# Recurrent layer: scans and gated products in hand-written order on VectorE, four copies moved to ScalarE and four casts to GpSimd

## The chip, the cores and the metric

The kernel runs on one NeuronCore of a Trainium2 chip. The metric is the device time of one execution in microseconds (us), median of repeated runs. The core has TensorE (PE; PEld is its weight loading), VectorE (DVE), ScalarE (ACT), GpSimd (POOL) and SyncE (SP, which here only issues DMAs). Each engine takes its own instructions strictly in order; semaphores hold an instruction until what it reads is written and what it overwrites is free.

## The reference, cut to what matters

Two residual layers on a sequence of 512 tokens by 1024 features: a hybrid layer (state space and attention), then the recurrent layer, each followed by a squared-ReLU MLP. The change lies in the recurrent layer alone:

```python
gate, xr = zf[..., :LRU_WIDTH], zf[..., LRU_WIDTH:]          # z = u @ rec_w_in
xc = conv(xr)                                                # width 4, depthwise
for direction in range(2):
    r = sigmoid(blockdiag(xc, ra_w[direction]) + ra_b[direction])
    i = sigmoid(blockdiag(xc, ix_w[direction]) + ix_b[direction])
    log_a = -LRU_C * r * softplus(-lam[direction])
    a = exp(log_a)
    b = sqrt(-expm1(2.0 * log_a)) * (i * xc)
    h = scan(a, b, reverse=(direction == 1))                 # h_t = a_t h_(t-1) + b_t
    hs.append(h)
y = (hs[0] + hs[1]) * gelu(gate)
mix = y @ rec_w_out
```

## The kernel before

Activations lie feature by token: a tile has 128 features (partitions) by 512 tokens, so the layer's 1024 features are eight tiles. Every matmul operand is split into a rounded part (`hi`, or `wh` for weights) and a remainder (`lo`, `wl`), and each product is three matmuls: wh times hi (L586), wh times lo (L587), wl times hi (L588); for the small gate products these are L559 to L561. A weight block `wr` of 128x1024 comes by DMA; `wtile` makes `wh` from it on the engine that `self.hi_eng` names at that moment (GpSimd, L520, or ScalarE, L522) and `wl` on VectorE (L523).

The layer works on two groups of four feature tiles, g = 0 and 1. For each tile: convolution (L1470 on GpSimd, then L1472 on VectorE), split (L1477 to L1480), four gate products on TensorE, ScalarE's Tanh, Exp, Tanh and Square (L1506 to L1513) and two VectorE steps (L1514, L1515). When the four tiles of a group are through, `roots` takes their square roots on ScalarE (L1528), which needs another table of functions than Tanh, and for each tile on VectorE: a product (L1530), a forward scan into `hs` (L1533), a backward scan in place into `ti` (L1534), their sum (L1535). `behind(...)` keeps ScalarE from starting the roots ahead of the last gate function of the fourth tile.

While this goes on, TensorE computes the other columns of the input projection. Those of the gate branch for group 0 stand in the four `ps` banks until `raw` takes them (four copies on VectorE, L1591); then `ps` is computed again for group 1's gate branch. `branch` applies Gelu on ScalarE (L1545). `merge` makes, for each of four tiles, the gated product on VectorE (L1554), its rounded copy on ScalarE (L1555, into a tile `a`) and the remainder on VectorE (L1556, into a tile `ti`). Two feature tiles share one `a` and one `ti`, and these are the buffers of group 1's scans: four of each exist, so the first pair of merged tiles can only be written when tile 0's scans of group 1 have been read, the second pair after tile 1, and so on.

The eight merged tiles, in four pairs `ys`, are the moving operands of the output projection `wout`. TensorE takes them pair by pair: one pair is a chunk of 24 matmuls (4 outputs x 2 tiles x 3), a first half of the outputs is 4 chunks, and the rest follows. The first pair is written `a_7800`, `ti_7801` in the program before and `a_7795`, `ti_7796` after it; the second `a_7808`, `ti_7809` and `a_7813`, `ti_7814`.

The order of each engine's instructions is set by a scheduler that knows an estimated duration of each; only inside `manual_schedule` is an engine's order that of the code. Before, the roots and merges are left to the scheduler.

Of the kernel before, what the change touches and what calls it, by code (L numbers as in the profile page):

```python
# [11 lines left out]
F32 = mybir.dt.float32  # L12
F32R = mybir.dt.float32r
I32 = mybir.dt.int32
AF = mybir.ActivationFunctionType
ALU = mybir.AluOpType
# [3 lines left out]
P = 128  # L20
# [40 lines left out]
class Kern:  # L61
# [1372 lines left out]
    def rglru(self, u, h, win, gw, wout, g1, s, sh):  # L1434
# [4 lines left out]
        with ExitStack() as ctx:  # L1439
# [84 lines left out]
            def roots(g, gt, after):  # L1524

                with behind(after):
                    for a, th, ti in gt:
                        last = (A.activation(th, th, AF.Sqrt, scale=0.25),)  # L1528
                for o, (a, th, ti) in enumerate(gt):
                    V.tensor_tensor(ti, ti, th, op=ALU.mult)  # L1530
                    hs = self.tl(rp, "hs", [P, 512], bufs=8)
                    a, ti = both(a), both(ti)
                    V.tensor_tensor_scan(hs, a[:, 0], ti[:, 0], 0.0, op0=ALU.mult, op1=ALU.add)  # L1533
                    V.tensor_tensor_scan(ti[:, 1, ::-1], a[:, 1, ::-1], ti[:, 1, ::-1], 0.0, op0=ALU.mult, op1=ALU.add)  # L1534
                    V.tensor_tensor(hs, hs, ti[:, 1], op=ALU.add)  # L1535
                    hfs[g * 4 + o] = hs
                return last
# [10 lines left out]
            def merge(g, gg):  # L1548

                for o in range(4):  # L1550
                    if o % 2 == 0:
                        hi2, lo2 = (both(self.tl(rp, t, [P, 1024], F32R, bufs=4)) for t in ("a", "ti"))
                    hi, lo = hi2[:, o % 2], lo2[:, o % 2]
                    V.tensor_tensor(tok(gg[o]), tok(gg[o]), perm(hfs[g * 4 + o]), op=ALU.mult)  # L1554
                    A.copy(hi, gg[o])  # L1555
                    V.tensor_tensor(lo, gg[o], hi.bitcast(F32), op=ALU.subtract)  # L1556
                    ys.append((hi, lo))
# [11 lines left out]
            for g in range(2):  # L1569
# [16 lines left out]
                if g == 0:  # L1586
                    xps = [fetch(4 + o, ps[o], None, None) for o in range(4)]
                    last = roots(0, gt, last)
            raw = [self.tl(rp, t, [P, 512], bufs=2) for t in ("xh", "xl") * 2]
            for o in range(4):  # L1590
                V.tensor_copy(raw[o], ps[o])  # L1591
            self.hi_eng = None
            ps = self.lin(win, u, 512)
            last = roots(1, gt, last)
            gg, last = branch(raw, last, raw)
            merge(0, gg)
            gg, last = branch(ps, last)
            merge(1, gg)
# [188 lines left out]
```

## Time and profile before

| | us |
|---|---|
| median of 3 runs (1228.93 to 1230.33) | 1229.25 |
| the profiled execution: its own time | 1232.16 |
| its span, first to last instruction | 1230.4 |
| PE busy / DVE / ACT / POOL in the span | 1156.2 / 790.8 / 538.9 / 167.3 |

The rows of the trace are in the section of rows below. Times in them are counted from the span's start. The recurrent layer runs from about 687 to 870 us; between 760 and 820 us TensorE has idle time, and its granted clock falls there, while it is busy nearly all of the time on both sides.

### The profile page before, as it was taken

How to read it: one execution, taken by the hardware profiler on the slowest of the kernel's cores; microseconds unless marked ns; L12 is line 12 of the kernel's file. 1: busy time of each engine (PE TensorE's matmuls, PEld its weight loads, DVE VectorE, ACT ScalarE, POOL GpSimd, SP SyncE). 2: the span in 40 equal slices, each digit the busy share in tenths (PEclk: the TensorE clock that was granted, in tenths of full speed). 3: DMA queues.
4: the chain of work that ended last, by engine and by line, in shares of the span. 5: the costliest groups of instructions: out<-in, count | busy, mean ns of one | idle time of the engine just before them, and what ended most of it. 6: DMA issues, size and time to landing. Idle time of an engine off the chain costs nothing.

```text
span 1230.4 us, 17016 instructions
## 1 busy us (share of the span) xinstructions
PE 1156.2 (94%) x6584; PEld 970.9 (79%) x6584; DVE 790.8 (64%) x1223; ACT 538.9 (44%) x929; POOL 167.3 (14%) x239
## 2 busy tenths in 40 slices
PE   4898889899999999999999998889999999999997
PEld 2687667668988888888889986669988888888886
DVE  6586988997789765486333799885744323344243
ACT  4356787663543412233323369934534211343230
POOL 2449883200000000000000261000000000000000
PEclk8998889999999999999999999889999999999999
DMA  9421020356277676475322422132232332332311
GB/s 351 159 65 61 23 73 32 130 172 229 70 251 260 208 239 204 145 251 187 101 87 69 138 86 69 35 98 72 86 105 88 101 103 89 100 103 87 102 35 69
DMA packets 85905, 151.76 MB, mean 123 GB/s; under 512 B 5696, under 2 KB 34368, under 8 KB 85824
## 3 DMA queue, kind: packets, MB, share of 16 engines
q1 hardware_dynamic: 85824, 150.67, 37.4%
q8 instruction: 51, 0.84, 0.3%
q14 instruction: 30, 0.25, 0.1%
HBM read 148.55 MB, written 2.10 MB: 122 GB/s over the span
## 4 chain that ended last, share of the span: by engine, by line
PE 75%; DVE 14%; ACT 5%; issue 2%; POOL 2%; DMA 1%; SPq 0%; DVEq 0%; POOLq 0%; ACTq 0%
PE ps L587 13%; PE ps L588 13%; PE ps L586 13%; PE px L586 8%; PE px L588 8%; PE px L587 8%; DVE wl L523 2%; PE p L748 1%; PE po L1045 1%; DVE ti L1534 1%; DVE actb L459 1%; DVE hs L1533 1%; ACT pexp L1028 1%; PE p L587 1%; PE p L586 1%
## 5 line engine op out<-in xcount | busy, mean ns | idle before, releaser
L523 DVE TENSOR_TENSOR wl<-wr,wh 128x1024 fp32r<-128x1024 f32 (+1 forms) x169 | 205.1, 1215 | 272.5 <-ACT wh L522 265.7
L522 ACT CAST wh<-wr 128x1024 fp32r<-128x1024 f32 (+1 forms) x161 | 165.8, 1030 | 419.9 <-PE ps L587 200.4
L587 PE MATMUL ps<-actb,wh 128*128 128x512 f32 (+1 forms) x512 | 181.3, 354 | 0.1
L586 PE MATMUL ps<-acta,wh 128*128 128x512 f32 (+1 forms) x328 | 116.6, 356 | 0.0
L588 PE MATMUL ps<-acta,wl 128*128 128x512 f32 (+1 forms) x328 | 116.3, 355 | 0.0
L586 PE MATMUL ps<-hid,wh 128*128 128x512 f32 x288 | 112.1, 389 | 0.0
L588 PE MATMUL ps<-hid,wl 128*128 128x512 f32 x288 | 112.0, 389 | 0.0
L587 PE MATMUL ps<-hid,wh 128*128 128x512 f32 x288 | 112.0, 389 | 0.0
L587 PEld LDWEIGHTS ps<-actb,wh 128*128 128x128 f32 x512 | 97.5, 190 | 13.4 <-DVE actb L905 0.3
L586 PE MATMUL px<-hid,wh 128*128 128x512 f32 (+1 forms) x288 | 98.9, 343 | 0.0
L587 PE MATMUL px<-hid,wh 128*128 128x512 f32 (+1 forms) x288 | 98.5, 342 | 0.0
L588 PE MATMUL px<-hid,wl 128*128 128x512 f32 (+1 forms) x288 | 98.5, 342 | 0.0
L587 PE MATMUL px<-actb,wh 128*128 128x512 f32 (+1 forms) x224 | 85.5, 382 | 0.0
L668 DVE SCALAR_TENSOR_TENSOR acc<-wr,cact,acc 128x1024 f32<-128x1024 f32 x49 | 62.8, 1282 | 20.1 <-DMA wr<-ada_w 19.8
L588 PEld LDWEIGHTS ps<-acta,wl 128*128 128x128 f32 x328 | 62.8, 191 | 8.5
L586 PEld LDWEIGHTS ps<-acta,wh 128*128 128x128 f32 x328 | 62.7, 191 | 8.4
L586 PE MATMUL ps<-actc,wh 128*128 128x512 f32 (+1 forms) x184 | 65.1, 354 | 0.0
L588 PE MATMUL ps<-actc,wl 128*128 128x512 f32 (+1 forms) x184 | 64.8, 352 | 0.0
L587 PEld LDWEIGHTS ps<-hid,wh 128*128 128x128 f32 x288 | 54.1, 188 | 11.3
L588 PEld LDWEIGHTS ps<-hid,wl 128*128 128x128 f32 x288 | 54.0, 188 | 11.2
L586 PEld LDWEIGHTS ps<-hid,wh 128*128 128x128 f32 x288 | 54.1, 188 | 11.2
L587 PEld LDWEIGHTS px<-hid,wh 128*128 128x128 f32 x288 | 54.6, 190 | 6.3
(524 smaller groups left out, 2582.8 us busy)
## 6 DMA issues: line engine op xcount, KB each, us to landing
wr<-w SPq DMA_DIRECT2D x128, 512.0 KB, 3.7
wr<-ada_w SPq DMA_DIRECT2D x56, 512.0 KB, 4.4
wr<-wout SPq DMA_DIRECT2D x16, 512.0 KB, 3.7
araw<-ada_w SPq DMA_DIRECT2D x32, 256.0 KB, 3.0
wr<-win SPq DMA_DIRECT2D x16, 512.0 KB, 3.8
wr<-win SPq DMA_DIRECT2D x8, 384.0 KB, 6.0
h<-xT SPq DMA_DIRECT2D x8, 256.0 KB, 6.2
acta<-ada_w SPq DMA_DIRECT2D x8, 256.0 KB, 5.6
```

What stands on the lines that cost most here:

```text
L459: V.tensor_tensor_scan(*z, 0.0, op0=ALU.mult, op1=ALU.add)
L522: nc.scalar.copy(hi, src)
L523: (lo_eng or nc.vector).tensor_tensor(lo, src, hi.bitcast(F32), op=ALU.subtract)
L586: mm(out, wh, xh, start=first and a == a0 and lead(o), stop=False, skip_group_check=True)
L587: mm(out, wh, xl, start=False, stop=False, skip_group_check=True)
L588: mm(out, wl, xh, start=False, stop=last and a == a0 + kk - 1, skip_group_check=True)
L668: nc.vector.scalar_tensor_tensor(acc, raw, self.ca[:, k:k + 1], acc, op0=ALU.mult, op1=ALU.add)
L748: self.nc.tensor.matmul(ps[o:o + 32, 0:raws[k].shape[1]], self.ca[:, k:k + 1].to_broadcast([P, 32]), raws[k], start=k < 4, stop=k >= 4, sk ...
L1028: self.exp = nc.scalar.activation(p, s, AF.Exp, bias=nb, scale=r, accum_out=self.esum[:, h, t:t + 1])
L1045: self.nc.tensor.matmul(po[h2 * 64:h2 * 64 + 64, t * 128:(t + 1) * 128], self.vp[:, kb, p // 2], pts[h2][:, kb * 128:(kb + 1) * 128], star ...
L1533: V.tensor_tensor_scan(hs, a[:, 0], ti[:, 0], 0.0, op0=ALU.mult, op1=ALU.add)
L1534: V.tensor_tensor_scan(ti[:, 1, ::-1], a[:, 1, ::-1], ti[:, 1, ::-1], 0.0, op0=ALU.mult, op1=ALU.add)
```

## The change

- `roots` no longer issues the square roots (they are now lines of their own, L1588 for group 0 and L1597 for group 1) and writes its VectorE steps inside `manual_schedule` for VectorE: tile by tile, product, scan, scan, sum, in this order. After each tile of group 1 it calls `merge` for one tile of group 0 that came one place earlier.
- `merge` does one tile a call. The fourth tile of group 0 and all four of group 1 are merged behind the loop, outside of the hand-written order.
- The four copies of `ps` into `raw` are on ScalarE (L1592) and not on VectorE (L1591).
- `self.lin(win, u, 512)` is called ahead of `self.hi_eng = None`, so the casts of its four weight blocks are made on GpSimd (L520) and not on ScalarE (L522).
- Group 0's Gelu is issued ahead of group 1's scans in the code.

```diff
-            def roots(g, gt, after):
-
-                with behind(after):
-                    for a, th, ti in gt:
-                        last = (A.activation(th, th, AF.Sqrt, scale=0.25),)
-                for o, (a, th, ti) in enumerate(gt):
-                    V.tensor_tensor(ti, ti, th, op=ALU.mult)
...
+            def roots(g, gt, then=lambda o: None):
+
+                with self.tc.manual_schedule(engines={mybir.EngineType.DVE}):
+                    for o, (a, th, ti) in enumerate(gt):
+                        V.tensor_tensor(ti, ti, th, op=ALU.mult)
+                        hs = self.tl(rp, "hs", [P, 512], bufs=8)
+                        a, ti = both(a), both(ti)
+                        V.tensor_tensor_scan(hs, a[:, 0], ti[:, 0], 0.0, op0=ALU.mult, op1=ALU.add)
+                        V.tensor_tensor_scan(ti[:, 1, ::-1], a[:, 1, ::-1], ti[:, 1, ::-1], 0.0, op0=ALU.mult, op1=ALU.add)
+                        V.tensor_tensor(hs, hs, ti[:, 1], op=ALU.add)
+                        hfs[g * 4 + o] = hs
+                        then(o)
...
-            def merge(g, gg):
...
+            def merge(g, gg, o):
+
+                if o % 2 == 0:
+                    hi2, lo2 = (both(self.tl(rp, t, [P, 1024], F32R, bufs=4)) for t in ("a", "ti"))
+                    ys.extend((hi2[:, i], lo2[:, i]) for i in range(2))
+                hi, lo = ys[g * 4 + o]
...
                 if g == 0:
                     xps = [fetch(4 + o, ps[o], None, None) for o in range(4)]
-                    last = roots(0, gt, last)
+
+                    with behind(last):
+                        for a, th, ti in gt:
+                            last = (A.activation(th, th, AF.Sqrt, scale=0.25),)
+                    roots(0, gt)
             raw = [self.tl(rp, t, [P, 512], bufs=2) for t in ("xh", "xl") * 2]
             for o in range(4):
-                V.tensor_copy(raw[o], ps[o])
+                A.copy(raw[o], ps[o])
+            ps = self.lin(win, u, 512)
             self.hi_eng = None
-            ps = self.lin(win, u, 512)
-            last = roots(1, gt, last)
+            with behind(last):
+                for a, th, ti in gt:
+                    last = (A.activation(th, th, AF.Sqrt, scale=0.25),)
             gg, last = branch(raw, last, raw)
-            merge(0, gg)
-            gg, last = branch(ps, last)
-            merge(1, gg)
+            roots(1, gt, lambda o: merge(0, gg, o - 1) if o else None)
+            gg2, last = branch(ps, last)
+            merge(0, gg, 3)
+            for o in range(4):
+                merge(1, gg2, o)
```

**First place: the end of group 1's gates.** GpSimd from the last weight cast that both programs have there (`wh` rounded weights, `gwh` rounded gate weights, `xc` and `h` a convolution's first step). Before:

```order
L520 TENSOR_SCALAR wh_7576<-wr_7575 128x1024
L1470 TENSOR_SCALAR xc_7425<-xp_7304,cols_sb 128x512
L1479 TENSOR_SCALAR gwh_7464<-gw_7294 128x512
L1470 TENSOR_SCALAR h_7501<-xp_7308,cols_sb 128x512
L1479 TENSOR_SCALAR gwh_7540<-gw_7423 128x512
L1479 TENSOR_SCALAR gwh_7605<-gw_7499 128x512
```

After:

```order
L520 TENSOR_SCALAR wh_7579<-wr_7578 128x1024
L1470 TENSOR_SCALAR xc_7428<-xp_7304,cols_sb 128x512
L1479 TENSOR_SCALAR gwh_7467<-gw_7294 128x512
L520 TENSOR_SCALAR wh_7656<-wr_7655 128x1024
L1470 TENSOR_SCALAR h_7504<-xp_7308,cols_sb 128x512
L1479 TENSOR_SCALAR gwh_7543<-gw_7426 128x512
L520 TENSOR_SCALAR wh_7686<-wr_7685 128x1024
L520 TENSOR_SCALAR wh_7716<-wr_7715 128x1024
L1479 TENSOR_SCALAR gwh_7608<-gw_7502 128x512
L520 TENSOR_SCALAR wh_7746<-wr_7745 128x1024
```

Four casts of 128x1024 are added, one ahead of the last convolution and three behind it.

TensorE at the last tile's four gate products (`xh_7506` and `xl_7507` before, `xh_7509` and `xl_7510` after, are the tile's two parts). Before:

```order
L559 MATMUL px_7611<-xh_7506,gwh_7605 128x512
L559 MATMUL px_7621<-xh_7506,gwh_7605 128x512
L559 MATMUL px_7626<-xh_7506,gwh_7605 128x512
L559 MATMUL pn_7616<-xh_7506,gwh_7605 128x512
L560 MATMUL px_7611<-xl_7507,gwh_7605 128x512
L561 MATMUL px_7611<-xh_7506,gwl_7606 128x512
L560 MATMUL pn_7616<-xl_7507,gwh_7605 128x512
L561 MATMUL pn_7616<-xh_7506,gwl_7606 128x512
L560 MATMUL px_7621<-xl_7507,gwh_7605 128x512
L561 MATMUL px_7621<-xh_7506,gwl_7606 128x512
L560 MATMUL px_7626<-xl_7507,gwh_7605 128x512
L561 MATMUL px_7626<-xh_7506,gwl_7606 128x512
```

After, where the other two products stand, 24 rows behind the first two:

```order
L588 MATMUL ps_7652<-acta_6600,wl_7657 128x512
L586 MATMUL ps_7652<-acta_6605,wh_7686 128x512
L559 MATMUL px_7629<-xh_7509,gwh_7608 128x512
L560 MATMUL px_7629<-xl_7510,gwh_7608 128x512
L561 MATMUL px_7629<-xh_7509,gwl_7609 128x512
L587 MATMUL ps_7652<-actb_6606,wh_7686 128x512
L588 MATMUL ps_7652<-acta_6605,wl_7687 128x512
L586 MATMUL ps_7652<-acta_6611,wh_7686 128x512
L559 MATMUL pn_7619<-xh_7509,gwh_7608 128x512
L560 MATMUL pn_7619<-xl_7510,gwh_7608 128x512
L561 MATMUL pn_7619<-xh_7509,gwl_7609 128x512
L587 MATMUL ps_7652<-actb_6612,wh_7686 128x512
```

The four products stood together ahead of the projection's matmuls; now `px_7614` and `px_7624` still do, and the other two are set among the projection's, so that `px_7629` ends with the 34th matmul from the first that reads `xl_7510` on.

**Second place: from the roots to the second pair of merged tiles.** ScalarE from the last gate functions on (`th` a root, `xh` and `xl` the gate branch of group 0, tiles 0 to 3 in the order xh, xl, xh, xl). Before:

```order
L1513 ACTIVATE tr_7609<-a_7631 128x1024
L1528 ACT_TABLE_LOAD
L1528 ACTIVATE th_7415<-th_7415 128x1024
L1528 ACTIVATE th_7491<-th_7491 128x1024
L1528 ACTIVATE th_7567<-th_7567 128x1024
L1528 ACTIVATE th_7632<-th_7632 128x1024
L1545 ACT_TABLE_LOAD
L1545 ACTIVATE xh_7640<-xh_7640 128x512
L1545 ACTIVATE xl_7641<-xl_7641 128x512
L1545 ACTIVATE xh_7642<-xh_7642 128x512
L1545 ACTIVATE xl_7643<-xl_7643 128x512
```

After:

```order
L1506 ACTIVATE ti_7613<-px_7629,rgc_1084_5386 128x512
L1597 ACT_TABLE_LOAD
L1597 ACTIVATE th_7418<-th_7418 128x1024
L1597 ACTIVATE th_7494<-th_7494 128x1024
L1597 ACTIVATE th_7570<-th_7570 128x1024
L1592 COPY xl_7646<-ps_7342 128x512
L1506 ACT_TABLE_LOAD
L1506 ACTIVATE ti_7613<-pn_7619,rgc_1084_5386 128x512
L1592 COPY xh_7645<-ps_7341 128x512
L1597 ACT_TABLE_LOAD
L1597 ACTIVATE th_7635<-th_7635 128x1024
L1543 ACT_TABLE_LOAD
```

One Tanh (`ti_7613<-pn_7619`) now stands among the roots, with two more table loads around it and two of the copies.

VectorE up to the row that completes the second pair (`ti_7809` before, `ti_7814` after; `xp` and `hs` are group 1's gate branch and scans). Before:

```order
L1533 SCALAR_TENSOR_TENSOR hs_7792<-a_7631,ti_7610 128x512
L1534 SCALAR_TENSOR_TENSOR ti_7610<-a_7631,ti_7610 128x512
L1556 TENSOR_TENSOR ti_7801<-xh_7640,a_7800 128x512
L1556 TENSOR_TENSOR ti_7801<-xl_7641,a_7800 128x512
L1535 TENSOR_TENSOR hs_7787<-hs_7787,ti_7545 128x512
L523 TENSOR_TENSOR wl_7906<-wr_7904,wh_7905 128x1024
L1554 TENSOR_TENSOR xp_7816<-xp_7816,hs_7777 128x512
L1556 TENSOR_TENSOR ti_7809<-xh_7642,a_7808 128x512
L1556 TENSOR_TENSOR ti_7809<-xl_7643,a_7808 128x512
```

After:

```order
L523 TENSOR_TENSOR wl_7942<-wr_7940,wh_7941 128x1024
L1533 TENSOR_TENSOR hs_7801<-hs_7801,ti_7548 128x512
L1552 TENSOR_TENSOR xl_7644<-xl_7644,hs_7324 128x512
L1552 TENSOR_TENSOR xp_7823<-xp_7823,hs_7801 128x512
L1554 TENSOR_TENSOR ti_7796<-xl_7644,a_7795 128x512
L1528 TENSOR_TENSOR ti_7613<-ti_7613,th_7635 128x1024
L1531 SCALAR_TENSOR_TENSOR hs_7809<-a_7634,ti_7613 128x512
L1532 SCALAR_TENSOR_TENSOR ti_7613<-a_7634,ti_7613 128x512
L1533 TENSOR_TENSOR hs_7809<-hs_7809,ti_7613 128x512
L1552 TENSOR_TENSOR xh_7645<-xh_7645,hs_7329 128x512
L1552 TENSOR_TENSOR xp_7825<-xp_7825,hs_7809 128x512
L1554 TENSOR_TENSOR ti_7814<-xh_7645,a_7813 128x512
```

The second pair's last tile (`xh_7645`, tile 2 of group 0) is now multiplied only behind the fourth tile's scans, where the code calls its `merge`; before, all four products of group 0 stood ahead of the third tile's scans. From the first product with a root of group 1 to the second pair's last remainder there are 27 rows before and 33 after.

## Rows read from the trace of the kernel before

**Rows 1.** TensorE's waits, 740 to 830 us: waiter <- releaser, sum, times, longest.

```profile
PE ps L587 <- DVE ti L1556: 4.4, 1, 4.4
PE pn L559 <- ACT ti L1506: 4.2, 1, 4.2
PE px L560 <- DVE xl L1480: 3.1, 1, 3.1
```

**Rows 2.** Stretches: length, busy PE, PEld, DVE, ACT, POOL (count), clock, DMA, GB/s.

```profile
760.00:770.00 10.00, 5.50 (x23) 3.90 (x22) 10.00 (x11) 8.53 (x13) 0.00 (x0) 1.00 0.17 52
...
810.00:820.00 10.00, 7.10 (x21) 5.65 (x22) 10.00 (x13) 1.24 (x2) 0.00 (x0) 0.66 0.45 151
```

**Rows 3.** VectorE in order of time, second half: start, us, line, operation [idle <-releaser].

```profile
791.25 2.36 DVE L1530 TENSOR_TENSOR ti<-ti,th 128x1024 f32<-128x1024 f32 x2 [1.15 <-ACT th L1528]
793.53 1.22 DVE L1533 TENSOR_TENSOR_SCAN hs<-a,ti 128x512 f32<-128x512 f32 x1
794.66 1.20 DVE L1534 TENSOR_TENSOR_SCAN ti<-a,ti 128x512 f32<-128x512 f32 x1
...
800.26 1.06 DVE L1554 TENSOR_TENSOR xh<-xh,hs 128x512 f32<-128x512 f32 x1
801.24 0.69 DVE L1535 TENSOR_TENSOR hs<-hs,ti 128x512 f32<-128x512 f32 x1
...
807.07 1.20 DVE L523 TENSOR_TENSOR wl<-wr,wh 128x1024 fp32r<-128x1024 f32 x1
...
812.75 0.69 DVE L1556 TENSOR_TENSOR ti<-xl,a 128x512 fp32r<-128x512 f32 x1
...
816.71 0.69 DVE L1556 TENSOR_TENSOR ti<-xl,a 128x512 fp32r<-128x512 f32 x1
```

**Rows 4.** TensorE in order of time, output projection, pair 1 and start of pair 2.

```profile
813.49 0.63 PE L588 MATMUL ps<-a,wl 128*128 128x512 f32 x1
813.92 0.63 PE L586 MATMUL ps<-a,wh 128*128 128x512 f32 x1
...
820.21 0.39 PE L586 MATMUL ps<-a,wh 128*128 128x512 f32 x1
820.43 0.39 PE L587 MATMUL ps<-ti,wh 128*128 128x512 f32 x1
```

**Rows 5.** VectorE in order of time, group 1's gates and the copies.

```profile
725.21 2.06 DVE L1514 SCALAR_TENSOR_TENSOR th<-tr,th 128x1024 f32<-128x1024 f32 x1
...
736.25 1.21 DVE L1514 SCALAR_TENSOR_TENSOR th<-tr,th 128x1024 f32<-128x1024 f32 x1
...
748.28 0.69 DVE L1480 TENSOR_TENSOR xl<-xc,xh 128x512 fp32r<-128x512 f32 x1
...
780.25 0.68 DVE L1480 TENSOR_TENSOR xl<-h,xh 128x512 fp32r<-128x512 f32 x1
780.86 0.68 DVE L1591 COPY xl<-ps 128x512 f32<-128x512 f32 x1
```

**Rows 6.** GpSimd in order of time: a cast alone, a cast beside VectorE, later steps.

```profile
701.70 1.05 POOL L520 TENSOR_SCALAR wh<-wr 128x1024 fp32r<-128x1024 f32 x1 [1.83 <-PE ps L587]
...
724.90 1.30 POOL L520 TENSOR_SCALAR wh<-wr 128x1024 fp32r<-128x1024 f32 x1 [1.88 <-PE ps L587]
...
748.54 1.07 POOL L1470 TENSOR_SCALAR h<-xp,cols_sb 128x512 f32<-128x512 f32 x1 [5.04 <-DVE ti L1515]
749.58 0.62 POOL L1479 TENSOR_SCALAR gwh<-gw 128x512 fp32r<-128x512 f32 x1
```

**Rows 7.** ScalarE in order of time: a cast, the table load, the roots, Gelu.

```profile
757.24 1.04 ACT L522 CAST wh<-wr 128x1024 fp32r<-128x1024 f32 x1
...
788.87 1.28 ACT L1528 ACT_TABLE_LOAD   x1
790.16 3.91 ACT L1528 ACTIVATE th<-th 128x1024 f32<-128x1024 f32 x4
...
795.38 0.64 ACT L1545 ACTIVATE xh<-xh 128x512 f32<-128x512 f32 x1
```

More of the change, by code (lines that the diff above doesn't have):

```diff
@@ L1522, in behind @@
                 return st
-            def roots(g, gt, after):
-                with behind(after):
-                    for a, th, ti in gt:
-                        last = (A.activation(th, th, AF.Sqrt, scale=0.25),)
-                for o, (a, th, ti) in enumerate(gt):
-                    V.tensor_tensor(ti, ti, th, op=ALU.mult)
[L1531 to L1537, printed above, removed]
+            def roots(g, gt, then=lambda o: None):
[9 more added lines that the diff above has]
+                        then(o)
             def branch(ps, after, gg=()):
@@ L1546, in branch @@
                 return gg, last
-            def merge(g, gg):
[L1550 to L1557, printed above, removed]
+            def merge(g, gg, o):
[3 more added lines that the diff above has]
+                hi, lo = ys[g * 4 + o]
+                V.tensor_tensor(tok(gg[o]), tok(gg[o]), perm(hfs[g * 4 + o]), op=ALU.mult)
+                A.copy(hi, gg[o])
+                V.tensor_tensor(lo, gg[o], hi.bitcast(F32), op=ALU.subtract)
             ys = []
```

## The prediction

> **What bounds the kernel now.** I read TensorE's waits between 740 and 830 us first: outside this stretch TensorE is busy nearly all the time, and the change touches nothing there. It waits for a handful of things, VectorE and ScalarE results all [rows 1]. The table of stretches then says which engine is late: in 760 to 770 us VectorE is busy 10.00 of 10.00 us while TensorE is busy 5.50, and in 810 to 820 VectorE is again full, with TensorE at 7.10 and a granted clock of 0.66 on average [rows 2]. So here VectorE sets the pace, ScalarE feeds it, and TensorE only returns to being the bound once the merged tiles reach the output projection.
>
> The second half of VectorE's work begins at 791.25, when the first root of group 1 arrives, and from there it runs without a gap: product, scans, gated products and remainders [rows 3]. The second pair of merged tiles is complete at 816.71 + 0.69 = 817.40. TensorE, which waited 4.4 us for the first pair [rows 1] and then worked it off at the half clock (0.43 us from matmul to matmul, 813.49 to 813.92, against 0.22 later), starts on the second pair at 820.21 [rows 4]. From 820.21 on it has no waits worth naming. The second pair thus had 820.21 - 817.40 = 2.8 us of slack. The time after 820.21 is matmul work that the change doesn't alter, so the question is one number: **when does TensorE start on the second pair after the change?**
>
> **The change part by part.** An instruction on VectorE begins some 0.08 us before the one ahead ends (793.53 against 791.25 + 2.36), so I cost each at its row's length less 0.08: product with a root 1.14, scan 1.13, gated product 0.98, sum 0.61, `wl` 1.12, remainder 0.61 [rows 3].
>
> *The order on VectorE.* From the first product with a root to the second pair there are 27 rows before. At these prices: 4 root products 4.56, 8 scans 9.0, 5 gated products 4.9, 3 sums 1.83, 3 `wl` 3.36, 4 remainders 2.44, together 26.1, and the trace has 817.40 - 791.25 = 26.15; the prices hold. After the change there are 33 rows: one late L1515 step (same form as L1514's, 1.13 [rows 5]), three more gated products 2.94 (three of group 1 now stand ahead), one more sum 0.61 and one more `wl` 1.12. That is **+5.8 us**. The tile-by-tile order serves tile 2 of group 0 last, behind the fourth tile's scans, though TensorE wants it second.
>
> *Copies and casts, and the start of the second half.* Both programs are alike on VectorE to the `xl` step at 748.28 [rows 5], which ends its turn at 748.88. The next landmark is the last `xl`, at 780.25 before. There 31 instructions lie between, 21 long ones at 1.13 and 10 short ones at 0.60, 29.7 us, against 31.4 traced, so 1.7 go to waits and disturbance. After, 25 lie between, 17 long and 8 short, 24.0 us. The four copies (0.60 each by L1591 [rows 5], 2.4 in all) are no longer VectorE's, though they stood behind this landmark and partly in idle time, so I count nothing for them; on ScalarE two stand ahead of the roots and two among them. ScalarE also loses four casts of 0.95 [rows 7].
>
> GpSimd gets these casts, three of them inside the stretch. A cast alone takes 1.05; beside VectorE, an L1514 step that began at 725.21 while a cast ran from 724.90 to 726.20 took 2.06 instead of the 1.21 of its like at 736.25 [rows 5, 6]. So a cast costs a busy VectorE between 0.85, as seen, and its own 1.05; I take 1.05, as VectorE is always queued here, 3.15 for three. The fourth runs beside sums and scans and adds up to 1.05, which I leave to the range.
>
> The Trainium skill, "SBUF — State Buffer", section "Who interferes with whom", says that a VectorE instruction with two SBUF inputs and a GpSimd instruction that reads SBUF lock each other out for the whole instruction. That rule speaks against moving casts to GpSimd here; the row agrees in kind (0.85 of a possible 0.99 of overlap), and by the rule the three casts cost their full 3.2 where the row alone would give 2.6.
>
> The last `xl` then starts at 748.88 + 24.0 + 1.7 + 3.15 = 777.7, some 2.5 earlier than before. That gain is given back on TensorE: in its new order `px_7629`, which the last Tanh ahead of the roots reads, ends only with the 34th matmul from there. TensorE starts about 0.75 after `xl` does (778.5) and has been idle, so part of the 34 runs at 0.43: 7 such give 9.0 us, 10 give 9.6. Tanh, table load and first root add 0.2 + 0.57 + 2.38 (788.87 to 791.25 [rows 3, 7]). That is 790.7 to 791.3. Laying all rows of the engines end to end by the same prices, with the waits for `a` buffers that this short sum omits (Exp of group 1 may not overwrite `a` before group 0's scan has read it), I get 792.4. I take 792.0, **+0.75** on 791.25.
>
> *Two more table loads.* After the first root ScalarE goes on with two roots, a copy, a load, a Tanh, a copy, a load, a root, a load and three Gelus before the tile that VectorE wants first (`xl_7646`). With 0.95 a root (3.91 for four), 0.5 a copy or Gelu (0.64 less the overlap), 0.57 a Tanh, just over these, and 1.29 a load (788.87 to 790.16) [rows 7], it is there 9.85 after the first root; VectorE gets there after 8.7. A new wait of **+1.1** on VectorE.
>
> "ScalarE: Activation LUTs" of the Trainium skill, section "What ACT_TABLE_LOAD costs", adds a drain of some 1.38 us to each load; before's row shows the root 0.01 after the load's end, no drain. By that page of the Trainium skill the wait would be 1.1 + 3 x 1.38 = 5.2, by the row 1.1.
>
> *Sum.* The second pair is complete at 817.40 + 5.8 + 0.75 + 1.1 = 825.05. Its first matmul wants only the rounded copy, and `xh_7645`'s product ends two rows ahead of the last remainder, so TensorE starts about 0.9 earlier, 824.1: 3.9 behind 820.21. Before that it idles twice (behind the halves of the first pair), so it meets the second pair at the half clock. In the trace 12 matmuls after such an idle ran at 0.43; I take 8, 8 x 0.2 = 1.6, between 0 and 2.4. **In all +5.5 us**: a span of 1235.9 where the profile shows 1230.4. The profiled execution took 1232.16 in all, 1.8 around its span and 2.9 over the median, so I carry the difference over: 1229.25 + 5.5 = **1234.8**. What this measurement can tell from no change is 0.2%, 2.5 us.
>
> **The rivals.** *GpSimd's casts cost VectorE nothing and the gates end early (ends on the other side: not slower).* Place: VectorE between 748.88 and the last `xl`. Without the 3.15, and with the 1.7 gone too, `xl` starts at 772.9, the second half at about 786.5, 5.5 earlier than I take, and the sum is 0: 1229.3. It decides from a start before 789.0. For it: ScalarE is relieved of 3.8 us. Against it: the 2.06 us row, and a fully busy VectorE.
>
> *Faster.* The same mechanism carried on: the root of group 1 comes before 783.5, the second pair is ready by 816, and TensorE, with 2.4 of lost clock and 1.3 of the 4.4 us wait gone, gets there at 820.2 - 3.7 = 816.5: about 1225.5. Against it: ScalarE's own chain of gates, with the `a` buffers bound to the scans, hardly leaves room.
>
> *ScalarE is later still.* Each of the three loads holds its successor by as much again as it takes (3 x 1.29 = 3.9 at the wait above): 1238.7. Nothing in the rows of before shows it. The drain of the Trainium skill's page "ScalarE: Activation LUTs", 1.38 a load, would come to 1239.0, an estimate.
>
> *The scheduler does not do what the code says.* The rows of the order for VectorE have the hand-written sequence, so this one is closed.
>
> **How the numbers follow.** Forecast, +3 to +9 us: 0.74. No change by the first rival: 0.13. Faster: 0.06. Late ScalarE: 0.07. The low end is the first rival's 1229.2; the high end takes a start at 793.5, the fourth cast's 1.05 and the full 2.4 of slow clock, 1238.5. Below the range lie the 0.06 and about half of the 0.13, above it about 0.06. Slower by over 0.2%: 0.74 + 0.07 + 0.01 of the first rival, 0.82; within: 0.12; faster: 0.06.
>
> **What would show it.** Right: `xl_7510` near 778; the first root product near 792; a VectorE wait for a Gelu of about 1 us near 801; the second pair's last remainder near 825; TensorE idle for over 5 us inside the first pair (its second tile waits for the third tile's scans) and again for some 2 us ahead of the second. Wrong: the second half starting before 789; VectorE steps of 1.2 us beside GpSimd's casts; TensorE starting the second pair before 821.

## The result and the profile after

The changed kernel takes **1235.14 us** (median of 5 runs, 1234.49 to 1237.18); the kernel before, run beside it, 1230.33. The ratio is 1.0052 with a 95% interval of 1.0042 to 1.0063: slower by half a per cent, as forecast (1234.8). The two medians alone differ by 4.8 us (0.39%), and 0.52% would be 6.4 us, so the size of the loss is known to some 1.5 us. The profiled execution took 1234.84 with a span of 1232.9.

The two profiled executions can't be laid on each other by their clocks. Up to the end of group 1's second split, VectorE and TensorE have the same instructions in both programs, yet the changed one got there earlier; that offset is scatter from a part that the change doesn't touch (in the fourteen traces of this document the common row named next falls anywhere between 735.77 and 742.03). So all times below are counted from one row that both have, the `xl` step before the one of [rows 5]. It, and the next one, on VectorE, before (start, duration, engine, line, operation, output <- inputs):

```profile
741.59 0.68 DVE L1480 TENSOR_TENSOR xl<-xc,xh 128x512 fp32r<-128x512 f32 x1
742.96 1.88 DVE L1472 SCALAR_TENSOR_TENSOR xc<-xp,cols_sb,xc 128x512 f32<-128x512 f32 x2 [0.69 <-POOL xc L1470]
```

and after, where GpSimd runs a weight cast beside the second row:

```profile
738.43 0.68 DVE L1480 TENSOR_TENSOR xl<-xc,xh 128x512 fp32r<-128x512 f32 x1
739.79 2.54 DVE L1472 SCALAR_TENSOR_TENSOR xc<-xp,cols_sb,xc 128x512 f32<-128x512 f32 x2 [0.68 <-POOL xc L1470]
```

The cast:

```profile
740.31 1.48 POOL L520 TENSOR_SCALAR wh<-wr 128x1024 fp32r<-128x1024 f32 x1
```

From that row I count some 380 matmuls, to the same one by number in the middle of the output projection; in each of the traces the stretch has 96 full-width matmuls of that projection and 63 or 64 of half the width, so it is the same work. The table of stretches has this once for before, once for after (start:end, length, busy time of PE, PEld, DVE, ACT and POOL with counts, granted clock, DMA share, GB/s):

```profile
741.59:844.10 102.51, 87.45 (x380) 70.61 (x380) 88.08 (x99) 68.36 (x94) 4.34 (x5) 0.92 0.21 70
```

```profile
738.43:846.57 108.14, 88.06 (x381) 70.17 (x380) 89.20 (x95) 69.01 (x96) 10.72 (x9) 0.92 0.20 66
```

The stretch is 5.63 us longer, the whole difference from that row to the end (488.8 and 494.5 us). TensorE's busy time is nearly the same, 87.45 and 88.06, so most of the loss is waiting: length less busy time is 15.06 before and 20.08 after. The waits that answer to [rows 1] (waiter <- releaser, sum, times, longest) say on whom:

```profile
PE ps L586 <- ACT a L1553: 9.7, 3, 6.3
PE pn L559 <- ACT ti L1506: 4.5, 2, 3.5
PE px L560 <- DVE xl L1480: 2.7, 1, 2.7
```

The first line is new: TensorE waits three times for rounded tiles `a` of the output projection. Before, its one long wait there was 4.4 us for remainders of the first pair [rows 1]. The rounding on ScalarE (L1553) is not what is late; it has itself waited 6.66 us for VectorE's gated product:

```profile
813.55 0.62 ACT L1553 CAST a<-xl 128x512 fp32r<-128x512 f32 x1 [6.66 <-DVE xl L1552]
```

VectorE's second half after, for [rows 3]:

```profile
774.51 0.68 DVE L1480 TENSOR_TENSOR xl<-h,xh 128x512 fp32r<-128x512 f32 x1
...
787.97 1.23 DVE L1528 TENSOR_TENSOR ti<-ti,th 128x1024 f32<-128x1024 f32 x1 [2.61 <-ACT th L1597]
789.23 1.22 DVE L1531 TENSOR_TENSOR_SCAN hs<-a,ti 128x512 f32<-128x512 f32 x1
790.37 1.20 DVE L1532 TENSOR_TENSOR_SCAN ti<-a,ti 128x512 f32<-128x512 f32 x1
791.61 0.69 DVE L1533 TENSOR_TENSOR hs<-hs,ti 128x512 f32<-128x512 f32 x1
...
798.16 1.10 DVE L1552 TENSOR_TENSOR xl<-xl,hs 128x512 f32<-128x512 f32 x1 [1.34 <-ACT xl L1543]
...
815.00 1.25 DVE L1528 TENSOR_TENSOR ti<-ti,th 128x1024 f32<-128x1024 f32 x1
816.29 1.23 DVE L1531 TENSOR_TENSOR_SCAN hs<-a,ti 128x512 f32<-128x512 f32 x1
817.43 1.20 DVE L1532 TENSOR_TENSOR_SCAN ti<-a,ti 128x512 f32<-128x512 f32 x1
818.66 0.69 DVE L1533 TENSOR_TENSOR hs<-hs,ti 128x512 f32<-128x512 f32 x1
819.27 1.05 DVE L1552 TENSOR_TENSOR xh<-xh,hs 128x512 f32<-128x512 f32 x1
820.24 1.08 DVE L1552 TENSOR_TENSOR xp<-xp,hs 128x512 f32<-128x512 f32 x1
821.23 0.70 DVE L1554 TENSOR_TENSOR ti<-xh,a 128x512 fp32r<-128x512 f32 x1
```

From the first root product to the second pair's last remainder (821.93) it takes 33.96 us, against 26.15 before. TensorE, at the second pair (it answers to [rows 4]; the number in brackets is the idle time ahead and what ended it):

```profile
814.22 2.08 PE L586 MATMUL ps<-a,wh 128*128 128x512 f32 x4 [6.32 <-ACT a L1553]
...
821.08 2.08 PE L586 MATMUL ps<-a,wh 128*128 128x512 f32 x4 [2.33 <-ACT a L1553]
```

It waits 6.32 us for the second tile of the first pair, which now stands behind the third tile's scans, and 2.33 for the second pair, and each time starts again at the half clock: 2.08 us for four matmuls, where a like group took 1.09 before:

```profile
818.82 1.09 PE L586 MATMUL ps<-a,wh 128*128 128x512 f32 x4
```

From 821.00 to 824.30 the granted clock after is 0.50. The two stretches of [rows 2], after:

```profile
760.00:770.00 10.00, 5.50 (x23) 4.00 (x22) 10.00 (x9) 8.54 (x13) 1.78 (x2) 0.98 0.33 105
...
810.00:820.00 10.00, 4.53 (x12) 3.29 (x12) 9.93 (x11) 0.62 (x1) 0.00 (x0) 0.66 0.35 114
```

VectorE is full in both as before; in the second TensorE is busy for 4.53 of 10.00 us where it was 7.10.

### The profile page after: what moved, and what is told of

It is laid out like the page before. It is cut to its first block, busy times and chain, and to the rows that moved or that the text cites. A ratio compares the mean times of both kernels' runs of the same rounds, so it can differ in the third digit from the quotient of the medians.

```text
span 1232.9 us, 17015 instructions
## 1 busy us (share of the span) xinstructions
PE 1154.6 (94%) x6584; PEld 969.4 (79%) x6584; DVE 787.5 (64%) x1219; ACT 539.9 (44%) x931; POOL 173.2 (14%) x243
## 4 chain that ended last, share of the span: by engine, by line
PE 70%; DVE 16%; ACT 6%; issue 3%; POOL 3%; DMA 2%; DVEq 0%; SPq 0%; POOLq 0%; ACTq 0%
PE ps L586 12%; PE ps L587 11%; PE ps L588 11%; PE px L586 8%; PE px L587 8%; PE px L588 8%; DVE wl L523 3%; DMA wr<-ada_w 1%; DVE xc L1472 1%; PE p L748 1%; ACT pexp L1028 1%; PE pn L855 1%; PE p L586 1%; PE p L587 1%; PE p L588 1%
## 5 line engine op out<-in xcount | busy, mean ns | idle before, releaser
L522 ACT CAST wh<-wr 128x1024 fp32r<-128x1024 f32 (+1 forms) x157 | 161.4, 1029 | 420.1 <-PE ps L587 199.5
L586 PE MATMUL ps<-acta,wh 128*128 128x512 f32 (+1 forms) x328 | 116.9, 357 | 0.1
L586 PE MATMUL ps<-hid,wh 128*128 128x512 f32 x288 | 112.2, 389 | 0.0
L586 PE MATMUL px<-hid,wh 128*128 128x512 f32 (+1 forms) x288 | 98.9, 343 | 0.0
L586 PEld LDWEIGHTS ps<-acta,wh 128*128 128x128 f32 x328 | 63.0, 192 | 9.0 <-ACT xl L1592 0.5
L586 PE MATMUL ps<-actc,wh 128*128 128x512 f32 (+1 forms) x184 | 65.1, 354 | 0.0
L586 PEld LDWEIGHTS ps<-hid,wh 128*128 128x128 f32 x288 | 54.1, 188 | 11.2
L588 PEld LDWEIGHTS px<-hid,wl 128*128 128x128 f32 x288 | 54.6, 190 | 6.3
```

The lines of the kernel that those rows point to most:

```text
L522: nc.scalar.copy(hi, src)
L586: mm(out, wh, xh, start=first and a == a0 and lead(o), stop=False, skip_group_check=True)
L588: mm(out, wl, xh, start=False, stop=last and a == a0 + kk - 1, skip_group_check=True)
```

## The experiments

The prediction had put most of the loss on one thing: the order on VectorE serves the second pair late. Theory 1 is that. Rival A puts it on GpSimd's casts, rival B on ScalarE's copies and table loads. The twelve runs take the three parts of the change apart (order, copies, casts), each alone, each left out, and then move the one place in the order that theory 1 blames. "Order" stands for all of the change that is neither copies nor casts: also the square roots as lines of their own and group 0's Gelu ahead of the scans, which no run takes apart. "Lost" below is the difference of medians to the kernel before on the same chip, with the 95% interval of the ratio. Ratio and medians differ by up to 1.6 us, and the traces, from the common row to the end of the span, lie up to 2 us off the medians (6.1 gained against 8.0 in the best kernel below). So nothing here is made to rest on less than 2 us.

### One part alone

**Order alone** (the changed kernel, copies and casts put back):

```
-                A.copy(raw[o], ps[o])
-            ps = self.lin(win, u, 512)
+                V.tensor_copy(raw[o], ps[o])
             self.hi_eng = None
+            ps = self.lin(win, u, 512)
```

> The changed kernel with the copies back on VectorE and the casts back on ScalarE: only the tile-by-tile order of VectorE is left. Theory (the order costs the time: 33 rows instead of 27 from the first product with a root to the second pair, 5.8 us): from that product to the second pair 32 us or more, as in the changed kernel (34.0), against 26.2 before, and the kernel 3 to 6 us slower than before. Rival A (casts on GpSimd hold VectorE) and rival B (copies and table loads hold ScalarE): the order by itself is free, the kernel within 1 us of before.

Measured: 1230.63 against 1228.63, ratio 1.0018 (1.0005 to 1.0032). 2.0 us lost, not the 3 to 6 that theory 1 expected, though the second pair comes 33.50 us after the first root product, as it expected.

**Casts alone** (before, with one line moved):

```
-            self.hi_eng = None
             ps = self.lin(win, u, 512)
+            self.hi_eng = None
```

> The kernel before with nothing but the four casts of the second half's weights moved to GpSimd. Theory (order): from the first product with a root to the second pair still about 26 us, the start of the second half within 2 us of before's 791.25, the kernel within 2 us of before. Rival A (the casts hold VectorE): the last xl step or the gates come 3 us or more later, and the kernel is 3 to 5 us slower, nearly all that the change costs. Rival B: no difference.

Measured: 1231.46, ratio 1.0020 (1.0008 to 1.0032). 2.8 us lost. The last `xl` step comes 41.82 us behind the common row (777.59), before 38.66: the casts hold VectorE for 3.16 us, and the rest shifts with it. Rival A's mechanism is real; the loss is just under the 3 to 5 us that it expected.

**Copies alone** (before, with one word changed):

```
-                V.tensor_copy(raw[o], ps[o])
+                A.copy(raw[o], ps[o])
```

> The kernel before with nothing but the four copies of the gate products moved from VectorE to ScalarE. Theory (order): VectorE loses 4 x 0.6 = 2.4 us that were partly idle, ScalarE gains about as much, the kernel within 1.5 us of before. Rival B (copies and the table loads that come with them hold the roots): the first product with a root 3 us or more later than 791.25, the kernel 3 to 6 us slower. Rival A: no difference.

Measured: 1235.49, ratio 1.0056 (1.0039 to 1.0073). 6.9 us lost, more than the whole change loses. ScalarE in this kernel, a copy, and the last tile's function that now waits longest:

```profile
771.89 0.61 ACT L1591 COPY xl<-ps 128x512 f32<-128x512 f32 x1
...
780.74 0.69 ACT L1506 ACTIVATE tr<-px,rgc 128x512 f32<-128x512 f32 x1 [3.26 <-PE px L561]
```

the same function before:

```profile
782.25 0.69 ACT L1506 ACTIVATE tr<-px,rgc 128x512 f32<-128x512 f32 x1 [1.00 <-PE px L561]
```

and TensorE's waits:

```profile
PE ps L587 <- DVE ti L1556: 10.3, 1, 10.3
PE ps L586 <- ACT a L1555: 5.8, 1, 5.8
```

The copies themselves are 0.6 us each and stand where ScalarE has room. What they change is the order that the scheduler gives the others. The copy at 771.89 frees a `ps` bank ahead of the last `xl` (775.81), where the copies on VectorE stood behind it (780.86 [rows 5]), and TensorE starts on the projection that refills the banks at 773.24. The last tile's gate products, which stood in one block on TensorE ahead of that projection, now have its matmuls ahead of them and between them: the first that reads the last `xl` starts 4.3 us behind it (780.09), before 0.7 us (780.99). So ScalarE waits 3.26 us for one, and the first root product comes at 53.29 instead of 49.66. And on VectorE the scheduler puts two more `wl` steps and a gated product ahead of the first pair's remainders: from the root product to the first of them 24.2 us (790.45 to 814.63) instead of 20.9 (791.25 to 812.17). TensorE, with the rounded halves of that pair in hand, waits 10.3 us for it.

So order alone costs less than half of the loss, and the part that the prediction counted as nothing costs the most. Theory 1 as the whole reason is gone, and rival B's signs came (the first root product 3.6 us later, and 6.9 us lost where it had 3 to 6), though the root waits for TensorE's matmuls and not for copies or table loads; theory 2, in the words of the next expectations, is that the parts act through each other.

### One part left out

**Copies and casts, without the order:**

> The kernel before with both the copies on ScalarE and the casts on GpSimd, VectorE's order left to the scheduler: the change without its order. Theory 1 (the prediction's: the tile-by-tile order is the loss): faster than the changed kernel by 3 us or more, within 2.5 us of before. Theory 2 (formed on the runs with one part alone: the copies on ScalarE make the scheduler place work ahead of the first pair's remainders and the roots late, 6.9 us, the casts add 2.5, and the hand-written order takes back a part): slower than the changed kernel, 8 to 12 us slower than before, with the first product with a root 5 us or more later than before and TensorE waiting 8 us or more for the first pair's remainders.

Measured: 1240.87 against 1228.84, ratio 1.0109 (1.0090 to 1.0128). 12.0 us lost, over twice the change's loss. The first root product comes at 57.17, and TensorE's waits are

```profile
PE ps L587 <- DVE ti L1556: 10.3, 1, 10.3
PE ps L586 <- ACT a L1555: 7.1, 1, 7.1
```

With copies and casts moved, the hand-written order is worth some 7 us. Theory 2 holds, with the loss at the upper end of its range.

**The change with the casts back on ScalarE** (as in the first diff, the last three lines):

> The changed kernel with the four casts back on ScalarE: order and copies are left. Theory 1 (order is the loss, casts cost VectorE 3.15 us that the earlier start hides in part): 3 to 5 us slower than before, since all terms of the second half stay. Theory 2 (each part is only as dear as the place where it falls): 0 to 2.5 us slower than before, so that the casts are most of what the change costs. By rows: GpSimd's casts gone, the steps beside them at 1.2 us instead of 1.5 to 2.1, the last xl step 2 us earlier.

Measured: 1232.44, ratio 1.0033 (1.0018 to 1.0048). 3.6 us lost, so the casts give back 1.2: that lies in theory 1's range (3 to 5) and outside theory 2's (0 to 2.5), a miss for theory 2, though the interval (2.2 to 5.9 us) does not exclude its upper end. The last `xl` step comes at 34.86 instead of 36.08 in the changed kernel, 1.2 earlier, not 2.

**The change with the copies back on VectorE:**

> The changed kernel with the four copies back on VectorE: order and casts are left. Theory 1: VectorE gets 2.4 us of copies that stand partly in its idle time, ScalarE loses four copies and perhaps two table loads: 4 to 6 us slower than before, as the changed kernel. Theory 2: 2 to 4 us slower than before, between the order alone (2.0) and order and casts added (4.5).

Measured: 1230.77, ratio 1.0026 (1.0010 to 1.0043). 1.9 us lost, just under theory 2's range (2 to 4) and well under theory 1's (4 to 6).

**The change with the roots behind all four Tanh of the last tile**, so that ScalarE loads tables twice less:

```
-                        sig = A.activation(...)
+                        sigs.append(A.activation(...))
...
-                return (a, th, ti), (sig, last)
+                return (a, th, ti), (*sigs, last)
```

> The changed kernel with the roots held behind all four Tanh of the last tile instead of one: ScalarE loads its function tables twice less (2 x 1.28 us) and the four roots stand together again. Theory 1 and 2 alike, by the step on table loads (two more loads cost 1.1 us of VectorE's waiting): the wait of 1.34 us for the Gelu of the first tile is gone, but the first product with a root comes some 2 us later, so the kernel stays within 1.5 us of the changed one. Rival B (the loads hold ScalarE): 2 to 3 us faster than the changed kernel.

Measured: 1234.13, ratio 1.0054 (1.0033 to 1.0076), the changed kernel's 1.0052 again. The first root product comes at 51.66 instead of 49.54, and the time to the second pair falls from 33.96 to 31.93, with 0.36 of waiting for the Gelu instead of 1.34. What the loads cost, the later roots cost as well: the counted stretch is 1.4 us shorter (106.77 against 108.14), and the 2 to 3 us of rival B's second half do not appear.

### The place of the merge

**All of group 0 merged behind the second tile's scans, the rest as in the change:**

```
-            roots(1, gt, lambda o: merge(0, gg, o - 1) if o else None)
+            roots(1, gt, lambda o: [merge(0, gg, i) for i in range(4)] if o == 1 else None)
             gg2, last = branch(ps, last)
-            merge(0, gg, 3)
```

> The changed kernel with one edit in VectorE's order: all four tiles of group 0 are merged straight behind the scans of the second tile of group 1, none is left for behind the fourth tile. Copies and casts stay where the change puts them. Theory (order): the second pair is complete some 20 to 25 us behind the first product with a root, not 34.0, TensorE meets it without the two idle times of 6.3 and 2.3 us, and the loss is gone: from 2 us faster to 1 us slower than before. Rivals A and B: the casts and copies are still there, so the kernel stays 4 to 6 us slower than before.

Measured: 1223.82 against 1228.63, ratio 0.9957 (0.9941 to 0.9973), 4.8 us **faster** than before, where theory 1 had 2 us at best and the rivals a loss. From the root product to the second pair 25.06 us, and the idle times of 6.3 and 2.3 us are gone.

**The same merge with copies and casts put back:**

> All of group 0 merged straight behind the second tile's scans, with copies back on VectorE and casts back on ScalarE. Theory 1 (the place of the second pair in VectorE's order is what counts): 4 to 7 us faster than before, and 6 to 9 us faster than the same kernel with the tile-by-tile merge (2.0 us slower than before). Theory 2 adds that copies and casts cost some 2 to 3 us more here too: so 1 to 3 us faster than the same order with the copies on ScalarE and the casts on GpSimd (4.8 faster than before). If copies and casts help this order: 3 us faster than before or less.

Measured: 1220.81 against 1228.84, ratio 0.9940 (0.9922 to 0.9957), 8.0 us faster, somewhat more than either theory expected. It is the best median here, though its interval overlaps those of both early merges with the copies moved. Its stretch of 380 matmuls:

```profile
740.35:834.27 93.92, 85.64 (x382) 68.16 (x381) 88.06 (x99) 67.60 (x94) 4.62 (x5) 0.95 0.22 71
```

8.28 us of waiting instead of 15.06. Not all of the 8.6 us gained here stays: in the 33 us that follow, the mean granted clock is 0.90 where it was 0.95 (two stretches, this kernel and then before):

```profile
834.27:867.89 33.62, 31.83 (x242) 31.65 (x241) 20.38 (x51) 14.07 (x27) 0.00 (x0) 0.90 0.25 78
```

```profile
844.10:876.13 32.03, 30.24 (x243) 30.07 (x241) 20.09 (x50) 14.02 (x27) 0.00 (x0) 0.95 0.22 67
```

1.6 us are given back to the half clock.

**With the copies moved, and with the casts moved:**

> The same early merge, copies on ScalarE, casts on ScalarE. Theory 2: between the early merge alone and the early merge with both, some 5 to 7 us faster than before; the casts then cost 0 to 2 us in this order. If the casts on GpSimd were a gain: 3 us faster than before or less.

Measured: 1223.30, ratio 0.9958 (0.9946 to 0.9969), 5.5 us faster, as expected.

> The same early merge, copies on VectorE, casts on GpSimd. Theory 2: 4 to 6 us faster than before, as with both; the copies by themselves are worth less than 2 us either way once the merge stands early, since they fall into VectorE's idle time ahead of the roots.

Measured: 1226.51, ratio 0.9984 (0.9974 to 0.9994), 2.3 us faster: a miss. Its profiled execution gained 5.5 us in the stretch and 4.2 to the end; why its median is less than that, the one trace doesn't show. The copies miss too: moving them gains 2.5 us with the casts on GpSimd (2.3 to 4.8) and costs 2.5 with the casts on ScalarE (8.0 to 5.5), not under 2 either way, and no run shows why the sign turns.

**One tile later:**

> Copies on VectorE, casts on ScalarE, and group 0 merged whole behind the third tile's scans, one tile later than the early merge. Theory 1: the second pair comes some 4.2 us (product, two scans, sum: 1.14 + 2.26 + 0.61, and a wait) later than with the early merge, the first pair too, so TensorE waits longer for both: 2 to 5 us slower than the early merge, and near the kernel before. Rival (the place does not matter, since TensorE finds other work): within 1 us of the early merge.

Measured: 1228.11, ratio 0.9998 (0.9987 to 1.0009), as before, and 7.3 us behind the merge one tile earlier, more than expected. Between the tile-by-tile merge and the early one the place is worth 10.0 us without copies and casts (2.0 lost, 8.0 gained), 9.6 with both, 9.1 with the copies and 4.2 with the casts.

### All runs in one table

Times in us from the common `xl` row; "length" and "waiting" are those of the 380 matmuls (waiting is length less TensorE's busy time in the table of stretches).

| kernel | last `xl` | first root product | second pair complete | length | waiting | lost, medians |
|---|---|---|---|---|---|---|
| before | 38.66 | 49.66 | 75.81 | 102.51 | 15.06 | |
| order | 34.87 | 48.80 | 82.30 | 104.61 | 13.58 | 2.0 |
| casts | 41.82 | 52.68 | 78.81 | 105.57 | 17.01 | 2.8 |
| copies | 38.65 | 53.29 | 81.59 | 109.38 | 22.01 | 6.9 |
| copies, casts | 41.79 | 57.17 | 85.49 | 112.09 | 26.46 | 12.0 |
| order, copies | 34.86 | 49.85 | 82.64 | 104.95 | 15.94 | 3.6 |
| order, casts | 36.07 | 50.42 | 83.02 | 104.75 | 16.39 | 1.9 |
| **order, copies, casts (after)** | 36.08 | 49.54 | 83.50 | 108.14 | 20.08 | 4.8 |
| after, Tanh first | 36.08 | 51.66 | 83.59 | 106.77 | 18.22 | 5.3 |
| early merge | 34.87 | 48.81 | 70.97 | 93.92 | 8.28 | -8.0 |
| early merge, copies | 34.85 | 49.85 | 74.91 | 95.95 | 10.02 | -5.5 |
| early merge, casts | 36.08 | 50.42 | 71.72 | 96.99 | 10.76 | -2.3 |
| early merge, copies, casts | 36.09 | 49.56 | 74.62 | 96.27 | 11.01 | -4.8 |
| merge after third tile | 34.85 | 48.77 | 77.92 | 101.48 | 12.11 | -0.7 |

Three readings. (1) The order brings the last `xl` step forward by 3.8 us, and with it the roots stay between 48.8 and 50.4 whatever copies and casts do; without it these add 3.0 and 3.6, and 7.5 together. (2) From the root product to the second pair the tile-by-tile order takes 6 to 8 us more than before in all its settings (31.9 to 34.0 against 26.15). (3) Yet order alone, with its second pair 6.5 us late, waits **less** on TensorE than before (13.58 against 15.06), and is yet 2.1 us longer: it is busy for 91.03 us instead of 87.45, at a mean granted clock of 0.90 instead of 0.92:

```profile
737.04:841.65 104.61, 91.03 (x382) 72.06 (x380) 88.63 (x99) 67.48 (x94) 4.61 (x5) 0.90 0.21 66
```

There the scheduler has set other matmuls ahead of the second pair, the half-width outputs `px` of the first. TensorE in the kernel with the order alone, 24 of them among the second pair's first four:

```profile
816.72 0.39 PE L586 MATMUL px<-a,wh 128*128 128x256 f32 x1 [0.75 <-ACT wh L522]
...
817.32 1.19 PE L586 MATMUL ps<-a,wh 128*128 128x512 f32 x4
...
821.41 0.28 PE L588 MATMUL px<-a,wl 128*128 128x256 f32 x1
821.53 0.40 PE L587 MATMUL ps<-ti,wh 128*128 128x512 f32 x1
```

It has work of the first pair up to the moment that the second is there. Both kernels with one part more have this fill too. The changed kernel has not: there the second pair's matmuls come directly and TensorE stands idle, and so it is with the roots behind all Tanh. The length is 104.6 to 105.0 with the fill, 106.8 and 108.1 without. That the fill makes this difference fits all five kernels, but no run changed it alone; why the scheduler chooses it or not is open.

## Why the prediction was right, and where its reason was not

**The bound: right.** VectorE sets the pace between the gates and the second pair, and the loss is TensorE's waiting for it.

**VectorE's order, +5.8: measured +6.5.** 33 rows, as counted, in 33.96 us less the 1.34 of waiting, against 26.15. Some 0.5 of the missing 0.7 is a price: a step that reads the result of the step directly ahead starts 1.26 and 1.29 behind a product (787.97 to 789.23, 815.00 to 816.29) and 1.24 and 1.23 behind a scan (790.37 to 791.61, 817.43 to 818.66), not 1.14 and 1.13. The 33 rows have four such links, the 27 rows before none.

**Start of the second half: last `xl` 2.6 earlier (forecast 2.5), first root product 0.1 earlier (forecast 0.75 later).** The casts' 3.15 in it was right as a sum and wrong in its parts. Three casts fall behind the row that the prediction counted from, and each costs what [rows 5, 6] showed, not the full 1.05. VectorE and GpSimd after, at the three:

```profile
749.29 2.06 DVE L1514 SCALAR_TENSOR_TENSOR th<-tr,th 128x1024 f32<-128x1024 f32 x1
...
753.67 1.52 DVE L1472 SCALAR_TENSOR_TENSOR h<-xp,cols_sb,h 128x512 f32<-128x512 f32 x1
...
765.69 2.05 DVE L1515 SCALAR_TENSOR_TENSOR ti<-ti,xc 128x1024 f32<-128x1024 f32 x1
```

```profile
748.80 1.48 POOL L520 TENSOR_SCALAR wh<-wr 128x1024 fp32r<-128x1024 f32 x1
...
753.06 1.60 POOL L520 TENSOR_SCALAR wh<-wr 128x1024 fp32r<-128x1024 f32 x1 [2.78 <-PE ps L587]
...
765.58 1.09 POOL L520 TENSOR_SCALAR wh<-wr 128x1024 fp32r<-128x1024 f32 x1 [2.00 <-PE ps L587]
```

2.06 instead of 1.21, 1.52 instead of 0.74 (743.39), and 2.05 instead of 1.21: 2.5 in all. The fourth cast, which the prediction put beside sums and scans and left to the range, lies ahead of that row, beside the 2.54 us shown at the top (before 1.88): 0.66. The two programs were alike in VectorE's instructions up to there, not in time. Counted from the prediction's own row, the last `xl` is 3.2 earlier, and that row itself is 0.7 late; that the two give the forecast 2.5 is luck. Together the casts cost 3.1, and the run with the casts alone has 3.16. Of the two prices that the prediction set side by side, the row's (0.85 of an overlap of 0.99) was nearer than the full hold that the Trainium skill's "SBUF — State Buffer", section "Who interferes with whom", states; in kind the page was right. The miss of 0.9 at the first root product is what the prediction added to its short sum for `a` buffers (792.0 for 790.7 to 791.3): from the last `xl` to the first root product it takes 13.46 us, and the short sum had 13.0 to 13.6.

**Two more table loads, +1.1: measured 1.34** (798.16). ScalarE's rows after show no drain, neither behind a load nor ahead of one, which the prediction had set against the 1.38 us of the Trainium skill's "ScalarE: Activation LUTs", section "What ACT_TABLE_LOAD costs":

```profile
785.58 1.28 ACT L1597 ACT_TABLE_LOAD   x1
786.88 2.96 ACT L1597 ACTIVATE th<-th 128x1024 f32<-128x1024 f32 x3
789.74 0.56 ACT L1592 COPY xl<-ps 128x512 f32<-128x512 f32 x1
790.32 1.28 ACT L1506 ACT_TABLE_LOAD   x1
791.62 0.69 ACT L1506 ACTIVATE ti<-pn,rgc 128x512 f32<-128x512 f32 x1
```

The measurement decides: 0.02 us from the copy's end to the load, and 0.02 from the load's end to the next function. The rival of a later ScalarE falls with it.

**TensorE starts on the second pair 3.9 later, and 1.6 more at the half clock: measured 4.0 and 1.6.** 82.65 against 78.62 from the common row (821.08 and [rows 4]'s 820.21). The reading of 820.21 was not exact: of the 24 matmuls from 807.06 on, ten are L586, where a pair has eight of each line, so at least two that read the second pair's rounded copies already stand in the group at 818.82, and the first pair's last is at 820.66. But 820.21 is the 25th matmul, as 821.08 is after, so the 4.0 is a delay at equal work. The eight matmuls from 821.08 to 824.50 then take 3.42 us, where eight at the full clock take 1.8 (0.23 each): that is the 1.6, and at the end of the counted stretch the delay is 5.63.

**Sum: +5.5 forecast, +5.6 in the traces, +4.8 in the medians.** Inside it the misses cancel: the start 0.9 less, the order 0.7 more, the loads 0.2 more; and 1234.8 comes so near to 1235.14 because the kernel before, run beside it, took 1230.33 and not 1229.25. Both are luck. The high end of the range is added up slightly wrong: 1234.8 + 1.5 + 1.05 + 0.8 is 1238.15, not 1238.5.

The signs came, if the changed trace is moved by the 3.16 us between the two common rows: the last `xl` at 777.7, the first root product at 791.1, the wait for a Gelu at 801.3, the last remainder at 825.1, idle times of 6.32 and 2.33. On its own clock the second half starts at 787.97, which the sign "before 789" would have taken for wrong. The rival of casts that cost nothing falls with the 3.16 us and the 2.8 us lost by casts alone, and the faster one with a start that is 0.1 earlier and not 7.8.

**What failed is the step on copies.** "I count nothing for them" looked for the copies' own time, 0.6 us each beside idle time. It is true that VectorE gains nothing. But moved alone they cost 6.9 us, and put back in the changed kernel they give back 2.9 (4.8 to 1.9), because they change the order in which the scheduler places TensorE's and VectorE's work. That this order is the reason is read from the rows of these kernels; no run moved the copies and held all engines' orders fixed. The prediction had half of it: it counted 34 matmuls until `px_7629` and set that against the earlier `xl`, but as a trait of the changed program, not as the price of the copies.

**The cause that the prediction named is the right place, but not the price of the order.** "The tile-by-tile order serves tile 2 of group 0 last": moving group 0's merges ahead of the third tile's scans and nothing else turns 4.8 us lost into 4.8 gained. Yet the order that it belongs to is not a loss as a whole: by itself it costs 2.0, and without it the kernel with copies and casts is 7 us slower still. Its good half (scans tile by tile: the last `xl` 3.8 us earlier, of which 0.9 reaches the first root product) and its bad half (the second pair late, 4 to 10 us by setting) are separate, and the early merge has only the good one.

## What to carry to other kernels

When a scheduler orders what isn't ordered by hand, price a moved instruction by the order that all engines get from it, not by its own time, and put a moved part back alone before naming it as the cause. Where an engine waits for tiles in a known sequence, write the producer's order by that sequence, here all four tiles of group 0 ahead of the third tile's scans, rather than by what is ready first. Times of two executions are best counted from a row that both share, and a stretch split into busy and waiting time of the bounding engine.

## What the runs showed of the hardware that was not expected

Beside VectorE's steps the cast on GpSimd can be held as well: 1.05 us alone [rows 6], 1.48, 1.60 and 1.09 in the rows above, 3.05 for one (758.91) in the kernel with the casts alone. The price of 0.10 to 0.15 us for a VectorE step that reads the one directly ahead was not foreseen either. And the half clock doesn't vanish when waiting goes: the early merge without copies and casts waits 6.8 us less in its stretch, and 1.6 us come back behind it at a mean granted clock of 0.90 instead of 0.95.
